# A decoder trunk in two layers on one core: 64 bytes of padding behind the constants, and with it every later tile in SBUF at another address

## The chip, the core and the metric

The kernel runs on one core of a Trainium2 chip. The metric is the device time of one execution in microseconds (us). The kernel before takes 2515.21 us, the median of three runs (2514.62 to 2516.56).

## What is computed

Two layers (DEPTH = 2) of a post-norm decoder over 256 tokens of width 2048, in float32:

```
h = x @ w_in                                  # 2048 -> 6704 columns
y = concat(hgrn2(h), nsa(h)) @ w_out          # two parallel head groups
x = LayerNorm(alpha * x + y)
f = (silu(gate) * up) @ w_down                # gate, up: causal depthwise conv of x @ w_up
x = LayerNorm(alpha * x + f)                  # w_up: 2048 -> 2*5632, w_down: 5632 -> 2048
```

Nearly all of the work is in the four products with weights. The two mixers (a gated linear recurrence and a sparse attention) run between the matmuls of `w_in`.

## The kernel before

Every weight is read from HBM once, in units of 128x1024 float32 (eight blocks of 128x128). SyncE loads a unit into `raw` (five buffers). ScalarE, or GpSimd for some units of `w_in`, rounds it to float32r as `whi` (`split`, L235 and L237), and VectorE writes the rest, `wlo` = `raw` - `whi` (L238); both have four buffers. Activations are held in the same two parts: `x` (16 blocks of 128x2x256), `o` (the mixers' outputs, in eight tiles of two blocks) and `f` (44 blocks). A block's first 256 columns are the high part and its next 256 the low part, so that they are 512 columns in a row.

`units` (from L300 on) makes the matmuls of one unit. For each of its eight blocks there is a matmul named **high** here (L325: 128x128 of `whi` as weights, all 512 columns of the activation's block moving) and one named **low** (L328: 128x128 of `wlo` as weights, the 256 columns of the high part moving):

```
mm(out, hi[:, o], x, start=k == 0, stop=False, ...)                        # L325, high
mm(st[c][:, 0], lo[:, 128 * i:128 * i + 128], act(k)[:, 0], ...)           # L328, low
```

Their order in a unit depends on `group`. In `w_up` and `w_down` it is 8: eight highs, then eight lows. In `w_in` and `w_out` it is 1: high, low, high, low. The first 12 units of `w_up` in each layer (6 column blocks, run side by side) have 2. The last column block of `w_out` and `w_down` takes two 256-column matmuls (L322) in place of a high. `w_in` has 80 such units a layer, `w_out` 32, `w_up` 176, `w_down` 88.

`tok_units` makes the value columns of `w_in` with the roles the other way round: 128x128 of `x` are the weights, and 512 columns (`w_v`) or 280 (`w_vg`) of `whi` or `wlo` move. It has three matmuls for each block and half of the tokens (L363, L364, L365), 12 a unit, and 16 units a layer of either width.

The order of the work on each engine, the buffers and the waits are settled when the program is built. Tiles come from pools that lie one behind the other in SBUF. The pool of constants holds `x`, `par`, `lbl`, `cf32`, `cb`, `lm`, `ones`, `eps`, `warm`, `half`, `lbt` and `lb`, in this order; a tile takes a multiple of 32 bytes of each partition. Behind it lies the pool of weights (`raw`, `whi`, `wlo`), and behind that the tiles of the stage: `o` and the mixers' work (`kh`, `q`, `hz` and others), or `f` and what the convolution and the norm need.

`lbt` is a small scratch tile in `load_consts`, used in a dozen short instructions at the start. Its rows 0 to 5 are used.

Of the kernel before, what the change touches and what calls it, by code (L numbers as in the profile page):

```python
# [29 lines left out]
F32 = mybir.dt.float32  # L30
# [73 lines left out]
class Trunk:  # L104
# [75 lines left out]
    def load_consts(self):  # L180
        nc, cp, a = self.nc, self.cp, self.a

        def ld(name, shape, dt):
            t = self.t(cp, shape, dt, name)
            self.after(nc.sync.dma_start(t, a[name]), self.load)
            return t

        self.after(self.load_par(0), self.load)
        self.lbl = ld("lbl", [128, L, 8], F32)
        self.cf = ld("cf32", [128, 673], F32)  # L190
        self.ident32 = self.cf[:, 641:673]
        self.cb = self.t(cp, [128, 416], BF16, "cb")
        self.lm = self.t(cp, [128, 80], U8, "lm")
        raw = self.t(self.wp, [128, 1024], F32, "raw", bufs=RAW_BUFS)
        self.after(nc.sync.dma_start(raw[:, :496], a["masks"]), self.load)
        nc.vector.tensor_copy(self.cb, raw[:, :416])
        nc.vector.tensor_copy(self.lm, raw[:, 416:496])
        self.ident = self.cf[:, 0:128]
        self.rc = self.cf[:, 128:384]
        self.rs = self.cf[:, 384:640]  # L200
        self.any = self.cf[:, 640:641]
        self.identb = self.cb[:, 0:128]
        self.caus = self.cb[:, 144:400]
        self.mask0 = self.cb[:, 128:416]
        self.ones = self.t(cp, [128, 128], F32, "ones")
        nc.gpsimd.memset(self.ones, 1.0 / D)
        self.eps = self.t(cp, [128, 3], F32, "eps")
        self.zero = self.eps[:, 2:3]
        nc.gpsimd.memset(self.zero, 0.0)
        self.warm = self.t(cp, [128, 1], F32, "warm")  # L210
        nc.gpsimd.memset(self.eps[:, 0:1], LN_EPS)
        nc.gpsimd.memset(self.eps[:, 1:2], RMS_EPS)
        self.half = self.t(cp, [128, 4], F32, "half")
        nc.gpsimd.memset(self.half, -0.5)

        v = nc.vector
        t = self.t(cp, [128, 6, 8], F32, "lbt")
        lb = self.lb = self.t(cp, [128, L, 2, 8], F32, "lb")
        v.tensor_max(t[:, 0], self.lbl[:, 0], self.lbl[:, 1])
        v.tensor_sub(t[:, 1], self.lbl[:, 0], t[:, 0])  # L220
        v.tensor_sub(t[:, 2], self.lbl[:, 1], t[:, 0])
        nc.scalar.activation(t[:, 1:3], t[:, 1:3], AF.Exp)
        v.tensor_add(t[:, 3], t[:, 1], t[:, 2])
        v.reciprocal(t[:, 3], t[:, 3])
        v.tensor_mul(t[:, 4], t[:, 1], t[:, 3])
        v.tensor_mul(t[:, 5], t[:, 2], t[:, 3])
        v.tensor_sub(lb[:, 0, 0], t[:, 4], t[:, 4])
        v.tensor_add(lb[:, 1, 0], t[:, 4], t[:, 5])
        v.tensor_sub(lb[:, 1, 0], lb[:, 1, 0], t[:, 4])
        for l in range(L):  # L230
            v.tensor_scalar(lb[:, l, 1], lb[:, l, 0], -1.0, 1.0, op0=ALU.mult, op1=ALU.add)
# [1109 lines left out]
```

## Time and profile before

| what | value |
|---|---|
| median of three runs | 2515.21 us (2514.62 to 2516.56) |
| the profiled execution's own time | 2517.57 us |
| its span, first to last instruction | 2515.8 us |
| mean granted TensorE clock | 0.993 of 2.4 GHz |
| TensorE matmuls (PE) busy | 2458.4 us, 98% of the span |
| weight loads (PEld) busy | 2121.2 us, 84% |
| VectorE (DVE) busy | 1781.0 us, 71% |
| ScalarE (ACT) busy | 1195.6 us, 48% |
| GpSimd (POOL) busy | 427.9 us, 17% |
| read from HBM | 432.20 MB, 173 GB/s over the span |

The profiled execution is 2.4 us above the median. PE's busy time joins matmuls that overlap in the pipeline, so a duration of one matmul says less than the distance from its start to the next one's start, which is what the timeline gives. In the timeline equal instructions that follow each other are one row with their count.

The stages of layer 0 lie at about 0 to 406 us (`w_in` with the mixers), 407 to 507 (`w_out` and the first norm), 513 to 998 (`w_up`) and 999 to 1247 (`w_down`); layer 1 repeats them about 1250 us later.

### The profile page before, as it was taken

To read this page: it belongs to the slowest core of one execution; us is meant where nothing else is said; L and a number is where in the kernel's file an instruction comes from. 1 tells how busy PE (TensorE), PEld (TensorE's weight loads), DVE (VectorE), ACT (ScalarE), POOL (GpSimd) and SP (SyncE) were. 2 spreads that over 40 slices of the span, in tenths; PEclk is the share of its full clock that TensorE was granted. 3 is DMA by queue.
4 is the path that set the end of the run, shared out by engine and by line. 5 is a ranking of instruction groups with operands and counts; after the bars stand their busy time and mean duration, and the time that the engine had idled before them with its cause. 6 is when DMAs were issued, how large, how long until landed. Compare 5 with 4: busy or idle time off the path is not lost.

```text
span 2515.8 us, 41290 instructions
## 1 busy us (share of the span) xinstructions
PE 2458.4 (98%) x15993; PEld 2121.2 (84%) x15993; DVE 1781.0 (71%) x2705; ACT 1195.6 (48%) x2189; POOL 427.9 (17%) x403
## 2 busy tenths in 40 slices
PE   8999999999999999999989999999999999999997
PEld 7788877888888888888878888788888888888887
DVE  7767876787777777555597678767977777775654
ACT  4144425465555555334331444354655555553343
POOL 0444551300000000001014445413000000000111
PEclk9999999999999999999999999999999999999999
DMA  6644343656666666665546443435565665655562
GB/s 234 212 156 142 119 147 122 184 168 193 192 190 190 192 192 192 186 191 185 159 156 206 154 135 126 142 127 176 176 193 190 190 191 192 193 188 190 178 199 101
DMA packets 122884, 436.99 MB, mean 174 GB/s; under 512 B 13760, under 2 KB 14528, under 8 KB 122688
## 3 DMA queue, kind: packets, MB, share of 16 engines
q1 hardware_dynamic: 122688, 434.35, 54.3%
q8 instruction: 126, 2.06, 0.3%
q14 instruction: 70, 0.57, 0.1%
HBM read 432.20 MB, written 2.10 MB: 173 GB/s over the span
## 4 chain that ended last, share of the span: by engine, by line
PE 87%; DVE 8%; issue 2%; ACT 1%; POOL 1%; DMA 1%; SPq 0%; ACTq 0%; POOLq 0%; DVEq 0%
PE pj L325 49%; PE pj L328 26%; DVE wlo L238 2%; PE pj L322 1%; PE pj L365 1%; PE pj L364 1%; PE t L325 1%; PE pj L363 1%; DVE rope L400 1%; PE h L657 1%; DMA raw<-w_in 1%; PE s L592 1%; PE s L513 1%; PE t L328 1%; DVE sg L447 1%
## 5 line engine op out<-in xcount | busy, mean ns | idle before, releaser
L238 DVE TENSOR_TENSOR wlo<-raw,whi 128x1024 fp32r<-128x1024 f32 (+2 forms) x819 | 1018.7, 1245 | 539.8 <-ACT whi L237 451.7
L325 PE MATMUL pj<-x,whi 128*128 128x512 f32 x3904 | 1117.7, 395 | 9.0 <-ACT whi L237 5.1
L237 ACT ACTIVATE whi<-raw 128x1024 fp32r<-128x1024 f32 (+2 forms) x631 | 661.7, 1049 | 796.1 <-PE pj L325 602.1
L325 PEld LDWEIGHTS pj<-x,whi 128*128 128x128 f32 x3904 | 709.0, 188 | 140.4 <-ACT whi L237 5.1
L328 PE MATMUL pj<-x,wlo 128*128 128x256 f32 x3904 | 715.6, 281 | 3.1 <-DVE wlo L238 3.1
L328 PEld LDWEIGHTS pj<-x,wlo 128*128 128x128 f32 x3904 | 592.1, 188 | 38.5 <-DVE wlo L238 4.4
L325 PE MATMUL pj<-f,whi 128*128 128x512 f32 x1320 | 331.2, 392 | 0.0
L235 POOL TENSOR_SCALAR whi<-raw 128x1024 fp32r<-128x1024 f32 (+1 forms) x188 | 217.7, 1160 | 330.9 <-PE pj L325 124.3
L325 PEld LDWEIGHTS pj<-f,whi 128*128 128x128 f32 x1320 | 237.3, 189 | 42.2
L828 POOL TENSOR_TENSOR s<-z 128x512 f32<-128x512 f32 x4 | 6.8, 1707 | 1182.2 <-DVE z L825 1182.2
L328 PEld LDWEIGHTS pj<-f,wlo 128*128 128x128 f32 x1408 | 191.7, 190 | 12.9
L328 PE MATMUL pj<-f,wlo 128*128 128x256 f32 x1408 | 197.6, 283 | 0.0
L1000 DVE SCALAR_TENSOR_TENSOR ct<-ch,par,ct 128x255 f32<-128x255 f32 (+1 forms) x352 | 167.8, 480 | 5.6
L325 PE MATMUL pj<-o,whi 128*128 128x512 f32 x480 | 168.5, 396 | 2.0 <-DVE o L600 1.9
L328 PE MATMUL pj<-o,wlo 128*128 128x256 f32 x512 | 143.5, 282 | 0.0
L325 PEld LDWEIGHTS pj<-o,whi 128*128 128x128 f32 x480 | 89.9, 188 | 23.8 <-DVE o L600 2.5
L998 ACT ACTIVATE ct<-ch,par 128x256 f32<-128x256 f32 x176 | 103.0, 587 | 0.0
L328 PEld LDWEIGHTS pj<-o,wlo 128*128 128x128 f32 x512 | 96.8, 189 | 0.4
L364 PE MATMUL pj<-wlo,x 128*128 128x280 f32 (+1 forms) x256 | 90.5, 355 | 5.6 <-DVE wlo L238 5.5
L363 PE MATMUL pj<-whi,x 128*128 128x280 f32 (+1 forms) x256 | 89.2, 355 | 2.3 <-POOL whi L235 2.3
L365 PE MATMUL pj<-whi,x 128*128 128x280 f32 (+1 forms) x256 | 90.7, 357 | 0.0
L375 DVE TENSOR_TENSOR ch<-pj,ch 128x256 f32<-128x256 f32 x170 | 70.9, 418 | 3.0 <-ACT ch L374 3.0
(248 smaller groups left out, 2249.2 us busy)
## 6 DMA issues: line engine op xcount, KB each, us to landing
raw<-w_up SPq DMA_DIRECT2D x352, 512.0 KB, 3.5
raw<-w_down SPq DMA_DIRECT2D x176, 512.0 KB, 3.6
raw<-w_in SPq DMA_DIRECT2D x158, 512.0 KB, 3.8
raw<-w_out SPq DMA_DIRECT2D x64, 512.0 KB, 3.6
raw<-w_v SPq DMA_DIRECT2D x32, 512.0 KB, 3.8
raw<-w_vg SPq DMA_DIRECT2D x32, 280.0 KB, 3.1
raw<-w_c SPq DMA_DIRECT2D x16, 512.0 KB, 3.6
out<-z SPq DMA_DIRECT2D x3, 512.0 KB, 2.6
```

Source lines behind the costliest of these rows:

```text
L235: self.nc.gpsimd.tensor_scalar(hi, raw, 1.0, 0.0, op0=ALU.mult, op1=ALU.add)
L237: self.nc.scalar.activation(hi, raw, AF.Copy)
L238: return self.nc.vector.tensor_sub(lo, raw, hi.bitcast(F32))
L322: mm(out[:, 0], hi[:, o], x[:, p], start=k == 0 and p == 0, stop=False, skip_group_check=True)
L325: mm(out, hi[:, o], x, start=k == 0, stop=False, skip_group_check=True)
L328: mm(st[c][:, 0], lo[:, 128 * i:128 * i + 128], act(k)[:, 0], start=False, stop=k == nk - 1, skip_group_check=True)
L363: mm(st[tt], xh, wh, start=first, stop=False, skip_group_check=True)
L364: mm(st[tt], xh, wl, start=False, stop=False, skip_group_check=True)
L365: mm(st[tt], xl, wh, start=False, stop=kt == KT - 1, skip_group_check=True)
L375: self.nc.vector.tensor_add(out, ps[:, 0], out)
L998: act(t[:, c], h[:, c], AF.Identity, scale=w[2], bias=w[3])
L1000: v.scalar_tensor_tensor(t[:, c, s:], h[:, c, :S - s], w[n], t[:, c, s:], op0=ALU.mult, op1=ALU.add)
```

## The change

The tile `lbt` gets two more rows that nothing reads or writes:

```
-        t = self.t(cp, [128, 6, 8], F32, "lbt")
+        t = self.t(cp, [128, 8, 8], F32, "lbt")
```

It grows from 192 to 256 bytes of each partition, so that every tile that is allocated behind it begins 64 bytes later. On each engine the instructions, their order and their waits are the same as before. Where the tiles begin, by the built program, in bytes of a partition:

| tile | before | behind a multiple of 128 by | after | behind a multiple of 128 by |
|---|---|---|---|---|
| `x` | 16512 | 0 | 16512 | 0 |
| `cf32` (with the identity) | 52832 | 96 | 52832 | 96 |
| `ones` | 56480 | 32 | 56480 | 32 |
| `raw`, first of five | 57408 | 64 | 57472 | 0 |
| `whi`, first of four | 77888 | 64 | 77952 | 0 |
| `wlo`, first of four | 94272 | 64 | 94336 | 0 |
| `o`, first tile, and `f` | 110656 | 64 | 110720 | 0 |
| `q`, first buffer | 198080 | 64 | 198144 | 0 |

The buffers of `raw`, `whi`, `wlo` and `o` are 4096 bytes each. A block of weights takes 512 bytes and a block of an activation 2048, so every block of a tile lies as its tile does against a multiple of 128. The distance from the weights to the moving columns, taken modulo 512 bytes, is 64 for `x` before and 0 after; for `o` and `f` it is 0 before and after.

## Rows read from the trace of the kernel before

**Rows 1.** The page: span, and each engine's busy us, share and instructions.
```profile
span 2515.8 us, 41290 instructions
PE 2458.4 (98%) x15993; PEld 2121.2 (84%) x15993; DVE 1781.0 (71%) x2705; ACT 1195.6 (48%) x2189; POOL 427.9 (17%) x403
```
**Rows 2.** The page: the chain that ended last, by engine, then by line.
```profile
PE 87%; DVE 8%; issue 2%; ACT 1%; POOL 1%; DMA 1%; SPq 0%; ACTq 0%; POOLq 0%; DVEq 0%
PE pj L325 49%; PE pj L328 26%; DVE wlo L238 2%; PE pj L322 1%; PE pj L365 1%; PE pj L364 1%; PE t L325 1%; PE pj L363 1%; DVE rope L400 1%; PE h L657 1%; DMA raw<-w_in 1%; PE s L592 1%; PE s L513 1%; PE t L328 1%; DVE sg L447 1%
```
**Rows 3.** Windows, layer 0: `w_out`, grouped part of `w_up`, `w_down`; columns in the first line.
```profile
core 0: us, PE busy (x) PEld busy (x) DVE busy (x) ACT busy (x) POOL busy (x), PEclk, DMA share, GB/s
...
407.00:507.00 100.00, 97.47 (x586) 85.01 (x585) 69.68 (x95) 46.11 (x59) 25.29 (x16) 1.00 0.54 168
...
546.00:998.00 452.00, 452.00 (x2623) 397.90 (x2622) 337.81 (x510) 267.18 (x424) 0.00 (x0) 1.00 0.61 192
1000.00:1247.00 247.00, 247.00 (x1461) 219.40 (x1460) 134.54 (x144) 98.65 (x99) 22.55 (x14) 1.00 0.60 187
```
**Rows 4.** Timeline, PE in `w_up`: start us, us to the last end, tiles, form, count.
```profile
701.14 1.99 PE L325 MATMUL pj<-x,whi 128*128 128x512 f32 x8
702.97 1.11 PE L328 MATMUL pj<-x,wlo 128*128 128x256 f32 x8
703.91 2.00 PE L325 MATMUL pj<-x,whi 128*128 128x512 f32 x8
705.75 1.07 PE L328 MATMUL pj<-x,wlo 128*128 128x256 f32 x8
706.65 1.99 PE L325 MATMUL pj<-x,whi 128*128 128x512 f32 x8
...
717.68 1.99 PE L325 MATMUL pj<-x,whi 128*128 128x512 f32 x8
```
**Rows 5.** Timeline, PE in `w_down`.
```profile
1102.21 2.00 PE L325 MATMUL pj<-f,whi 128*128 128x512 f32 x8
1104.05 1.12 PE L328 MATMUL pj<-f,wlo 128*128 128x256 f32 x8
1105.01 2.00 PE L325 MATMUL pj<-f,whi 128*128 128x512 f32 x8
...
1118.97 2.00 PE L325 MATMUL pj<-f,whi 128*128 128x512 f32 x8
```
**Rows 6.** Groups of weight loads: line, tiles, form, count, busy us, mean ns, idle.
```profile
L328 PEld LDWEIGHTS pj<-x,wlo 128*128 128x128 f32 x3904 | 592.1, 188 | 38.5 <-DVE wlo L238 4.4
...
L328 PEld LDWEIGHTS pj<-f,wlo 128*128 128x128 f32 x1408 | 191.7, 190 | 12.9
```
**Rows 7.** Timeline, PE in `w_out`: two highs, three pairs apart.
```profile
450.15 0.40 PE L325 MATMUL pj<-o,whi 128*128 128x512 f32 x1
...
451.21 0.40 PE L325 MATMUL pj<-o,whi 128*128 128x512 f32 x1
```
**Rows 8.** Timeline, PE in `w_in`: two highs, three pairs apart.
```profile
250.22 0.40 PE L325 MATMUL pj<-x,whi 128*128 128x512 f32 x1
...
251.28 0.40 PE L325 MATMUL pj<-x,whi 128*128 128x512 f32 x1
```
**Rows 9.** Timeline, PE in `w_v`: two matmuls, ten starts apart.
```profile
140.06 0.39 PE L365 MATMUL pj<-whi,x 128*128 128x512 f32 x1
...
142.40 0.39 PE L363 MATMUL pj<-whi,x 128*128 128x512 f32 x1
```
**Rows 10.** Groups by form: the first of three matmul lines of `tok_units`, both widths.
```profile
L363 PE MATMUL pj<-whi,x 128*128 128x512 f32 x128 | 52.3, 409 | 0.0
...
L363 PE MATMUL pj<-whi,x 128*128 128x280 f32 x128 | 36.9, 302 | 2.3 <-POOL whi L235 2.3
```
**Rows 11.** Groups of VectorE in `w_down`: an addition that reads `x`, one that does not.
```profile
L825 DVE SCALAR_TENSOR_TENSOR z<-x,z 128x256 f32<-128x256 f32 x8 | 3.4, 423 | 0.1
...
L824 DVE TENSOR_TENSOR z<-pj,z 128x256 f32<-128x256 f32 x8 | 3.4, 421 | 0.1
```

## The prediction

> **What bounds the kernel now.** I read the page first. The span is 2515.8 us and PE is busy for 98% of it [rows 1]. The chain that ended last says the same: 87% of it is PE, 49% the highs on `pj` (L325) and 26% the lows (L328), and only 8% is VectorE [rows 2]. So what counts is how closely matmuls follow each other. The windows show where nothing but that counts: in the grouped part of `w_up` and in `w_down` PE is busy for the whole stretch at a granted clock of 1.00, while VectorE is busy for 338 of 452 and 135 of 247 us, and the DMA engines for 0.61 and 0.60 of the time [rows 3]. Nothing else is late there, so a nanosecond more in the distance of two matmuls is a nanosecond more in the kernel.
>
> Then the timeline, for the distances. In `w_up` six groups of eight highs and eight lows take 717.68 - 701.14 = 16.54 us, 2.757 each [rows 4]. In `w_down` six groups take 1118.97 - 1102.21 = 16.76 us, 2.793 each [rows 5]. The instructions are of the same form in both, the weights come from the same buffers, the order in a group is the same, and PE waits for nothing in either. Yet a group costs 0.037 us more with `f` than with `x`. The lows differ most. With `x`, eight lows take 703.91 - 702.97 = 0.94 us in one group and 706.65 - 705.75 = 0.90 in the next [rows 4]; with `f` they take 0.96 [rows 5]. Their weight loads take 188 ns on average with `x`, and 190 with `f` [rows 6].
>
> Both the moving columns and the next weights are read from SBUF at the same time, and between the two stages only where the moving columns lie has changed: `x` lies 64 bytes from the weights (modulo 512), `f` 0 bytes. I take from this that the two reads get in each other's way, by an amount that hangs on their distance. That is a reading of two stages, not yet a proof.
>
> **The change part by part.** It adds no instruction, moves none and changes no wait. What it changes is addresses, and I go through who reads them.
>
> *w_up.* `x` stays and the weights move by 64 bytes, so that `x` comes to lie against its weights as `f` lies against them now, at distance 0. I price a group of `w_up` at a group of `w_down`: + 0.22 / 6 = 0.0367 us. There are 176 - 12 = 164 units in groups of eight a layer, 328 in all: 328 x 0.0367 = **+ 12.0 us**. All of it is on the path, as PE never idles there. The 24 units in groups of two have no counterpart with `f` or `o`; at the same 0.037 either way they are worth 0.9 us at most, and I take 0.
>
> *w_down.* `f` and the weights move together and their distance stays 0: **0 us**. If it is the place of `f` itself that costs, up to 0.037 a group comes back; that is a rival below.
>
> *w_out and w_in.* In `w_out` (distance 0) three pairs of high and low take 451.21 - 450.15 = 1.06 us [rows 7]; in `w_in` (distance 64) three pairs take 251.28 - 250.22 = 1.06 us [rows 8]. With highs and lows in turn the distance makes no difference that the rows show: **0 us**, with 0.01 us on three pairs either way, which over the 1280 pairs of `w_in` in both layers is 4.3 us.
>
> *The value columns.* Here `x` gives the weights and `whi` or `wlo` moves; the distance is 64 before, 0 after. Ten matmuls of 512 columns take 142.40 - 140.06 = 2.34 us, 0.234 each [rows 9]. At distance 0 the nearest row is the highs of `w_down`: 1104.05 - 1102.21 = 1.84 us for eight, 0.230 each [rows 5]. 3 x 128 matmuls of that width [rows 10] by 0.004 us are 1.5 us less; the 384 of 280 columns, priced by their width, 0.8 less. I take **- 2 us**. The bounds are 0 and - 3, the latter with the highs of `w_up`, 0.229 each [rows 4].
>
> *Everything else.* In the scores, the sums with `v` and the recurrence, both operands move together. The transposes and the sums with `ones` read one operand that stays, but they are few hundreds of short matmuls; I take 0, give or take 1 us. VectorE and ScalarE show no such effect: an addition that reads `x`, at a multiple of 128, takes 423 ns, and one of the same size that does not read it 421 [rows 11]. The loads into `raw` lie elsewhere too. No row shows one at a multiple of 128, but their queue has 0.39 of its time free in `w_up` [rows 3] and they run ahead of the work: 0 us, and the cover would have to go entirely before they cost anything.
>
> The sum is + 12 - 2 = **+ 10 us**. On the profiled execution that is 2517.57 + 10 = 2527.6; the median of the runs is 2.4 lower, so I forecast **2525 us**, with a range of its own of 2519 to 2531 (4.3 us for `w_in`, 0.9 and 1 for the small terms, and 1 for the value columns, of which I expect some to cancel).
>
> **Where the Trainium skill speaks against it.** The rows show matmuls of one form at distances that differ by stage, and weight loads that differ by 2 ns with them [rows 4 to 6]. The Trainium skill, in "SBUF — State Buffer", section "Who interferes with whom", says that TensorE has two read ports, one for the moving operand and one for weight loads, independent of each other, and that PE never waits on anyone. By that rule the sum is 0 and the time stays. The trace of before does not agree with it, as far as the difference of 0.037 us a group is one of addresses; no run so far moves an address alone.
>
> **The rivals.**
>
> *No change* (15%): the difference between `w_up` and `w_down` is not one of addresses, but of something else in which the stages differ, such as the place in the pattern at which a column block ends (16 blocks against 44) or VectorE's load, 75% against 54% [rows 3]. For it speaks that `w_in` and `w_out` cost the same [rows 7, 8] although their distances differ; against it, that the busier stage is the faster one. It gives 2515 us. The rule of the skill above gives the same.
>
> *The moving columns' own place counts* (18%): they are better read from a multiple of 128, as `x` is now, and the weights' place does not matter. Then `w_up` stays, and `w_down` gets its distance: 165 units (the last column block of 5.5 units a layer left out) x 0.0367 = 6.1 us less. The value columns come to 0.229 instead of 0.234: 384 x 0.005 = 1.9 less, and 1.0 for the narrower. That is - 9, 2506 us. For it: the value columns are at 64 behind a multiple of 128 and slow [rows 9], as `f` is. Against it: `o` is no slower than `x`.
>
> *Both aligned, hardly any conflict* (12%): no stage has both operands at a multiple of 128 now, so a state that no row shows is possible. Its best is bounded by the best of each kind: eight highs in 1.83 and eight lows in 0.90 [rows 4], a group at 2.73. `w_up` then gains 328 x 0.027 = 8.9 us, `w_down` 165 x 0.063 = 10.4, and the some 1790 pairs of `w_in` and `w_out`, from 0.353 to 0.342 (2.73 / 8), 20; the value columns 3. That is - 42, 2473 us.
>
> *A worse state* (12%): the same, on the other side. Highs as in the value columns, whose weights lie at a multiple of 128, 0.234 [rows 9], and lows as with `f`, 0.120 [rows 5], make a group of 2.83. `w_up` loses 328 x 0.073 = 24 us and `w_down` 165 x 0.037 = 6; a pair of `w_in` would be 0.354 and stay. That is + 30, 2545 us.
>
> **How the numbers follow.** The forecast has 43%. Its sign is decided in `w_up`: a group has to come out over 2.757 us by more than 0.015 for the kernel to be slower by 5 us, which is 0.2% and about what a measurement of this kernel can tell from no change. The range of 2502 to 2545 us takes in the forecast, no change, the moving columns' place and the worse state, and leaves out the 12% of a state without conflicts and some of the edges. Faster by over 0.2%: the 12% and most of the 18%, 0.28. Within 0.2%: the 15% and the edges of two others, 0.20. Slower: the forecast's rest and the worse state, 0.52.
>
> **What would show it.** If I am right, the timeline of `w_up` shows groups of 2.79 us with lows of 0.96, as `w_down` does before and after, and the weight loads of L328 with `x` rise from 188 to 190 ns; `w_in` and `w_out` keep 1.06 us for three pairs. If `w_down` falls to 2.757 and `w_up` stays, it was the moving columns' place. If a group of either stage lies below 2.74, distance is the wrong quantity altogether, and the place of the weights counts. If any difference shows on VectorE or in the loads rather than in PE's distances, the whole argument is beside the point.

## The result and the profile after

The changed kernel takes 2530.67 us, the median of four runs (2530.42 to 2533.06); the kernel before took 2515.23 beside it, also in four runs (2514.62 to 2516.56). The ratio is 1.0059, with a 95% interval of 1.0046 to 1.0071: slower by 0.59%, or 15.4 us (11.6 to 17.9 by the interval). The profiled execution took 2533.06 us, 2.4 above the median, as the profiled one of before did; it is the slowest of the four, with a granted clock of 0.990 where the other three have 0.992. Profile to profile the difference is 2531.3 - 2515.8 = 15.5 us, and it can be divided by stage. From the first matmul of a stage to the first of the next, and for `w_down` to the start of its own last matmul (us):

| stage | before, layer 0 | after | before, layer 1 | after | both layers |
|---|---|---|---|---|---|
| `w_in` | 401.54 | 404.84 | 400.98 | 402.71 | + 5.0 |
| `w_out` and first norm | 106.76 | 106.52 | 108.29 | 106.52 | - 2.0 |
| `w_up` | 485.43 | 491.64 | 485.43 | 491.64 | + 12.4 |
| `w_down` | 249.20 | 249.19 | 249.20 | 249.19 | 0.0 |

The page gives the same picture as [rows 1, 2]: the same instructions, the share of each engine the same to within 1%, and PE busier by 11 us.

```profile
span 2531.3 us, 41290 instructions
...
PE 2469.8 (98%) x15993; PEld 2135.7 (84%) x15993; DVE 1780.1 (70%) x2705; ACT 1196.4 (47%) x2189; POOL 428.1 (17%) x403
...
PE 87%; DVE 8%; issue 2%; DMA 1%; POOL 1%; ACT 1%; SPq 0%; ACTq 0%; POOLq 0%; DVEq 0%
```

VectorE, ScalarE and GpSimd are busy for the same time as before to within 1 us, so the addresses do nothing to them that the profile shows. The windows of `w_out`, of the grouped part of `w_up` and of `w_down` in layer 0 (columns as in [rows 3]) show the full clock, and in the last two a PE that never idles:

```profile
411.00:511.00 100.00, 97.15 (x585) 84.78 (x583) 70.00 (x96) 45.86 (x58) 25.23 (x16) 1.00 0.52 165
552.00:1002.00 450.00, 450.00 (x2580) 396.03 (x2579) 330.88 (x499) 261.87 (x415) 0.00 (x0) 1.00 0.60 190
1005.00:1252.00 247.00, 247.00 (x1450) 218.88 (x1449) 134.89 (x145) 100.39 (x103) 22.54 (x14) 1.00 0.58 186
```

The number of matmuls is the one to read: before, 452 us of `w_up` held 2623 of them, 5.80 a microsecond [rows 3]; now 450 us hold 2580, 5.73.

The timeline of PE in `w_up`, then in `w_down`:

```profile
700.93 2.00 PE L325 MATMUL pj<-x,whi 128*128 128x512 f32 x8
702.77 1.12 PE L328 MATMUL pj<-x,wlo 128*128 128x256 f32 x8
703.72 2.00 PE L325 MATMUL pj<-x,whi 128*128 128x512 f32 x8
705.56 1.12 PE L328 MATMUL pj<-x,wlo 128*128 128x256 f32 x8
706.52 2.00 PE L325 MATMUL pj<-x,whi 128*128 128x512 f32 x8
...
717.69 0.63 PE L325 MATMUL pj<-x,whi 128*128 128x512 f32 x2
...
1117.14 2.00 PE L325 MATMUL pj<-f,whi 128*128 128x512 f32 x8
1118.98 1.12 PE L328 MATMUL pj<-f,wlo 128*128 128x256 f32 x8
1119.93 2.00 PE L325 MATMUL pj<-f,whi 128*128 128x512 f32 x8
...
1133.90 1.32 PE L325 MATMUL pj<-f,whi 128*128 128x512 f32 x5
```

Six groups of `w_up` take 717.69 - 700.93 = 16.76 us, where they took 16.54 [rows 4]; six of `w_down` take 1133.90 - 1117.14 = 16.76, as before [rows 5]. `w_up` has become what `w_down` was: highs in 1.84 us, lows in 0.95. Over all 328 such groups the mean went from 2756.7 to 2793.2 ns, and the 158 of `w_down` stay at 2793.1. 328 x 0.0365 = 12.0 us of the 12.4; the other 0.4 are the units in groups of two. The weight loads of the lows with `x` went from 188 [rows 6] to 191 ns:

```profile
L328 PEld LDWEIGHTS pj<-x,wlo 128*128 128x128 f32 x3904 | 602.7, 191 | 35.9 <-DVE wlo L238 3.2
...
L328 PEld LDWEIGHTS pj<-f,wlo 128*128 128x128 f32 x1408 | 191.7, 190 | 12.9
```

In the three following pairs of timeline rows, three pairs of high and low in `w_out`, three in `w_in`, and ten value columns:

```profile
449.67 0.39 PE L325 MATMUL pj<-o,whi 128*128 128x512 f32 x1
...
450.71 0.39 PE L325 MATMUL pj<-o,whi 128*128 128x512 f32 x1
...
249.22 0.39 PE L325 MATMUL pj<-x,whi 128*128 128x512 f32 x1
...
250.26 0.39 PE L325 MATMUL pj<-x,whi 128*128 128x512 f32 x1
...
142.82 0.40 PE L363 MATMUL pj<-whi,x 128*128 128x512 f32 x1
...
145.11 0.39 PE L364 MATMUL pj<-wlo,x 128*128 128x512 f32 x1
```

1.04 us in both for three pairs, against 1.06 [rows 7, 8], and 2.29 us for ten value columns, against 2.34 [rows 9]. The matmuls of `w_in` follow each other a little more closely, and yet `w_in` is 5 us longer in this pair of executions. The windows show where the time lies: first the kernel after, then the kernel before.

```profile
60.00:80.00 20.00, 17.11 (x95) 14.43 (x94) 19.22 (x23) 6.58 (x14) 8.46 (x7) 0.90 0.69 222
100.00:120.00 20.00, 18.20 (x108) 15.38 (x107) 14.04 (x16) 2.52 (x8) 9.50 (x7) 0.91 0.71 231
140.00:160.00 20.00, 20.00 (x128) 16.41 (x128) 15.74 (x40) 14.29 (x45) 9.03 (x11) 0.93 0.44 139
360.00:380.00 20.00, 16.07 (x148) 11.93 (x151) 14.83 (x26) 6.82 (x22) 6.19 (x6) 0.83 0.34 108
```
```profile
60.00:80.00 20.00, 17.70 (x114) 14.88 (x111) 19.21 (x22) 6.28 (x14) 9.87 (x8) 1.00 0.69 225
100.00:120.00 20.00, 18.29 (x115) 15.29 (x114) 16.13 (x17) 2.90 (x9) 10.08 (x9) 1.00 0.70 238
140.00:160.00 20.00, 20.00 (x128) 15.91 (x128) 15.28 (x40) 15.01 (x49) 10.09 (x12) 1.00 0.48 155
360.00:380.00 20.00, 16.26 (x139) 12.07 (x140) 15.30 (x32) 7.00 (x23) 6.73 (x7) 0.91 0.38 123
```

A granted clock of 0.90 over 20 us is a stretch at 1.2 instead of 2.4 GHz, and (1 - 0.90) x 20 = 2.0 us is the most that it can cost. Together with the windows from 40 to 60 us (0.93 after, 0.91 before) and from 120 to 140 (0.98 and 1.00) that is at most 10.4 us after and 3.6 before, 6.8 more in layer 0. The lower clock stands behind places where PE had waited for its operands. The first place in the timeline at which the two kernels differ in this, after and before:

```profile
67.83 0.58 PE L328 MATMUL pj<-x,wlo 128*128 128x256 f32 x1 [2.90 <-DVE wlo L238]
```
```profile
67.48 0.39 PE L328 MATMUL pj<-x,wlo 128*128 128x256 f32 x1 [2.30 <-DVE wlo L238]
```

After a wait of 2.90 us the matmul takes 0.58 us, at half clock; after one of 2.30 it takes 0.39, at the full clock. The length of a wait does not decide it alone: early in `w_out` the kernel before has the same four waits in both layers, the longest 0.9 us, and a stretch at half clock among them in layer 1 only. In `w_in` of layer 1 both add to the time, the clock and the waits: at most 1.7 us more at the half clock, and 18.0 us without a matmul in `w_in`, where there were 14.1. Waits of PE between 1255 and 1660 us after, then between 1248 and 1654 before:

```profile
PE pj L325 <- POOL whi L235: 5.7, 2, 5.0
...
PE s L513 <- ACT o L517: 2.5, 2, 1.9
```
```profile
PE pj L325 <- POOL whi L235: 2.9, 2, 2.5
...
PE s L513 <- ACT o L517: 0.9, 2, 0.6
```

### The profile page after: what moved, and what is told of

Read it like the earlier page. It is cut to its first block, busy times and chain, and to the rows that moved or that the text cites. A ratio compares the mean times of both kernels' runs of the same rounds, so it can differ in the third digit from the quotient of the medians.

```text
span 2531.3 us, 41290 instructions
## 1 busy us (share of the span) xinstructions
PE 2469.8 (98%) x15993; PEld 2135.7 (84%) x15993; DVE 1780.1 (70%) x2705; ACT 1196.4 (47%) x2189; POOL 428.1 (17%) x403
## 4 chain that ended last, share of the span: by engine, by line
PE 87%; DVE 8%; issue 2%; DMA 1%; POOL 1%; ACT 1%; SPq 0%; ACTq 0%; POOLq 0%; DVEq 0%
PE pj L325 49%; PE pj L328 26%; DVE wlo L238 2%; PE pj L322 1%; PE t L325 1%; PE pj L364 1%; PE pj L365 1%; PE pj L363 1%; DVE rope L400 1%; PE h L657 1%; DMA raw<-w_in 1%; POOL whi L235 1%; PE s L592 1%; PE s L513 1%; DMA raw<-w_vg 1%
## 5 line engine op out<-in xcount | busy, mean ns | idle before, releaser
L328 PE MATMUL pj<-x,wlo 128*128 128x256 f32 x3904 | 725.0, 284 | 2.9 <-DVE wlo L238 2.9
L328 PEld LDWEIGHTS pj<-x,wlo 128*128 128x128 f32 x3904 | 602.7, 191 | 35.9 <-DVE wlo L238 3.2
```

## The experiments

Distance means the start of the activation's block minus the start of the weights, modulo 512 bytes. Each kernel has the same 41290 instructions; only tiles move. Each was timed beside the kernel before on the same chip (2517.82, 2516.84, 2518.2 and 2518.11 us in the four sessions: medians of 9 runs in the first and 13 in the last, one run in the other two). A time without a number of runs is that of one run. Times of stages and groups come from one profiled execution of each kernel. "Group" is the mean, in ns, over all 328 groups of eight highs and eight lows in `w_up`, or 158 in `w_down`.

**1. Both operands, or the distance between them?** The change moved the weights *and* set the distance of `x` to 0. `x` gets 64 unused bytes ahead of it, which moves it and all that lies behind; the second kernel adds the change itself.

```
-  self.x = self.t(self.cp, [128, KT, 2, S], F32R, "x")
+  self.x = self.t(self.cp, [128, 16 + KT * 2 * S], F32R, "x")[:, 16:].rearrange("p (k h t) -> p k h t", h=2, t=S)
```

Weights at a multiple of 128 as after, `x` 64 behind, distance 64 (`x` only moved):

> Everything behind and including x lies 64 bytes later than in the kernel before: the weights lie at a multiple of 128 as in the changed kernel, x at 64 behind one, and the distance from weights to x is 64 again. Theory of the distance: w_up goes back to 2.757 us a group with lows of 0.94 and 0.90, w_down stays at 2.793, about 2515 us. Theory of the weights' place: w_up stays at 2.793 as in the changed kernel, about 2530 us. Theory of x's place (a multiple of 128 is better for what moves): w_up at 2.79 or above, 2530 us or more.

Measured: 2515.84 us, `w_up` 485.43 and 485.47 us, group 2756.7; `w_in` 401.35 and 401.25 us, as before the change.

`x` and weights both 64 behind a multiple of 128, distance 0 (`x` moved, `lbt` with 8 rows):

> x lies 64 bytes later than in the kernel before and the weights 128 later, so that both are at 64 behind a multiple of 128 and the distance is 0. Theory of the distance: w_up at 2.793 us a group, as in the changed kernel, about 2530 us. Theory of the weights' place: w_up at 2.757, about 2515 us. With the run before it, all four pairs of places have then been seen.

Measured: 2531.99 us, `w_up` 491.67 us in both layers, group 2793.2; `w_in` 403.57 and 401.82 us. A group of each in the timeline, `x` only moved first:

```profile
700.20 1.99 PE L325 MATMUL pj<-x,whi 128*128 128x512 f32 x8
702.02 1.11 PE L328 MATMUL pj<-x,wlo 128*128 128x256 f32 x8
702.97 1.31 PE L325 MATMUL pj<-x,whi 128*128 128x512 f32 x5
```
```profile
700.01 2.00 PE L325 MATMUL pj<-x,whi 128*128 128x512 f32 x8
701.85 1.11 PE L328 MATMUL pj<-x,wlo 128*128 128x256 f32 x8
702.80 1.55 PE L325 MATMUL pj<-x,whi 128*128 128x512 f32 x6
```

2.77 us and 2.79; one group alone shows it badly, as its cost at distance 64 alternates, and the mean over 328 shows it well. With the two kernels of the case this makes four corners: weights at 64 or 0, `x` at 64 or 0. The cost goes with the distance in all four, and with neither place. The weights' place and the activation's place both fall as causes.

**2. The same in `w_down`.** `f` gets 64 bytes ahead of it (the same edit as for `x`, at the line that makes `f`); with it moves only what its stage allocates behind it.

> The kernel before with f alone moved by 64 bytes (and what its stage allocates behind it). Theory of the distance: w_down falls from 2.793 to 2.757 us a group, 165 groups x 0.0367 = 6 us less, 2509 us, faster than both kernels; w_up stays. If it were the stage that makes w_down slower (where column blocks end, VectorE's load), it stays at 2.793 and the time at 2515 us.

Measured: 2510.32 us, median of six (2508.53 to 2511.95), 0.9967 of the kernel before (0.9955 to 0.9980). `w_down` takes 246.00 us a layer, 3.2 less, and its group 2757.0; `w_up` stays at 485.43. This kernel is faster than both. A group of `w_down`:

```profile
1104.02 1.99 PE L325 MATMUL pj<-f,whi 128*128 128x512 f32 x8
1105.85 1.11 PE L328 MATMUL pj<-f,wlo 128*128 128x256 f32 x8
1106.79 0.39 PE L325 MATMUL pj<-f,whi 128*128 128x512 f32 x1
```

The tile that moves is now the activation, and the price of 64 bytes is the same, 0.036 us a group. The rival by which the stages differ in something else than addresses has fallen with this.

**3. Which distances are cheap?** `x` 32 and `f` 96 (`lbt` with 7 rows, 96 bytes ahead of `f`):

> Weights 32 bytes later than in the kernel before, f 96 behind its place against them: distance 32 for x, 96 for f, 0 for o. No theory has a number for these. If only 64 bytes matter, w_up and w_down each show either 2.757 or 2.793 us a group; if the effect is finer, other sums of lows and highs show up, between 2.72 (no conflict) and 2.84. Together with no change of w_out, 2495 to 2545 us.

Measured: 2540.00 us; `w_up` 492.68 us with a group of 2800.0, `w_down` 251.96 with 2826.5. `x` -64 and `f` 128 (`lbt` with 10 rows, 128 bytes ahead of `f`):

> Weights 128 bytes later than in the kernel before, f a further 128: the distance is -64 for x and 128 for f. If only the distance modulo 128 counts, every group is as before: w_up 2.757 us (highs 227.5, 230.4, 228.8 ns in turn), w_down 2.793, about 2516 us. If it counts modulo 256 or more, both stages show sums not seen yet.

Measured: 2524.49 us; group 2773.3 with `x`, 2810.1 with `f`. -64 and 64 differ by 128 bytes and by 17 ns, 0 and 128 by 17 ns as well: the pattern does not repeat after 128 bytes. `x` 48 and `f` 16 (16 bytes ahead of each):

> Distance 48 for x and 16 for f, 0 for o: x begins 16 bytes later in its tile, the weights 32 later, f 16 later in its tile. So far a group costs 2.793 us at 0, 2.800 at 32, 2.757 at 64 and 2.837 at 96. If the cost runs smoothly with the distance, 48 gives about 2.78 and 16 about 2.80. If 16 bytes decide, values outside of 2.75 to 2.84 turn up, perhaps under 2.757, which would be a better place than any seen.

Measured: 2536.95 us; group 2806.7 with `x`, 2786.2 with `f`. `x` -16 and `f` 80 (16 bytes ahead of `x`, `lbt` with 8 rows, 80 ahead of `f`):

> Distance -16 (112) for x and 80 for f, 0 for o: x begins 16 bytes later in its tile, the weights 96 later, f 80 later in its tile. If the cost runs smoothly with the distance, 112 gives about 2.815 us a group and 80 about 2.80, some 2535 to 2545 us in all. If 16 bytes decide, other values, perhaps under 2.757.

Measured: 2531.35 us; group 2806.7 with `x`, 2799.8 with `f`. In order of distance, eight highs and eight lows apart (ns):

| distance | -64 | -16 | 0 | 16 | 32 | 48 | 64 | 80 | 96 | 128 |
|---|---|---|---|---|---|---|---|---|---|---|
| highs | 1861.7 | 1865.8 | 1840.7 | 1853.1 | 1866.8 | 1863.3 | 1831.3 | 1849.1 | 1867.4 | 1861.2 |
| lows | 911.7 | 940.8 | 952.5 | 933.1 | 933.2 | 943.3 | 925.4 | 950.7 | 959.1 | 948.8 |
| group | 2773.3 | 2806.7 | 2793.2 | 2786.2 | 2800.0 | 2806.7 | 2756.7 | 2799.8 | 2826.5 | 2810.1 |

There is no smooth course. Distance 64, where `x` lay before, is the cheapest of the ten; each shift tried here that took `x` away from it made `w_up` longer. Where an expectation has another price for one of these distances (2.837 us a group at 96, lows of 0.907 at -64, highs of 1.845 at 0), the table is the mean over all groups and the better number.

**4. A distance of its own for highs and lows.** Highs are cheapest at 64, lows at -64. A gap of 64 bytes between the buffers of `whi` and of `wlo` (and `lbt` with 8 rows) gives `x` 0 to `whi` and -64 to `wlo`, and `f` and `o` 64 to `whi` and 0 to `wlo`. For the lows of `x` the expectation has the sign wrong: against the kernel before, `wlo` moves by 128 bytes and `x` stays, and 64 - 128 = -64.

> 64 bytes more ahead of whi, and 64 more between whi and wlo: for x the distance is 0 to whi and 64 to wlo, for f and o 64 to whi and 0 to wlo. If each kind of matmul pays by the distance to its own weights: w_up 1.841 for the highs as at distance 0 and 0.925 for the lows as at 64, a group at 2.765; w_down 1.831 and 0.953, at 2.784; about 2517 us. If the highs leave a state to the lows, the sums differ from these by 0.01 us or more.

Measured: 2527.06 us; group 2780.1 with `x` (lows 942.5) and 2790.4 with `f` (lows 951.1). The lows of `x`, at -64, did not get the 912 ns that they take where the highs are at -64 too: after highs at distance 0 they are dearer. What pays is `w_out`, with 104.65 us in place of 106.76: most pairs take 340 ns (340.7 on average), where the average before was 350. `w_in` was slow, 407.43 us in layer 0, with more of the half clock than in any other kernel.

Next, each stage its own place inside buffers that are 512 bytes longer. Room for them came from a smaller scratch of the DMA queues, so that `x` and all behind it lie 8192 bytes lower and the weights' buffers 4608 apart, both multiples of 512. 64 unused bytes ahead of `o` and ahead of `f` bring these to distance 64 as well. `AT` has the places of `whi` and `wlo` in their buffers, in elements of 4 bytes: 0 leaves the distance at 64, 16 makes it 0, and 32 makes it -64.

```
+AT = dict(w_in=(0, 16), tok=(16, 16), w_out=(0, 16), w_up=(0, 32), w_down=(16, 32))
...
-                    hi = self.t(self.wp, [128, 1024], F32R, "whi", bufs=PART_BUFS)
-                    lo = self.t(self.wp, [128, 1024], F32R, "wlo", bufs=PART_BUFS)
+                    hi, lo = (self.t(self.wp, [128, ROOM], F32R, tag, bufs=PART_BUFS)[:, a:a + 1024]
+                              for tag, a in zip(("whi", "wlo"), units[ns][3].__defaults__[-1]))
```

> Each stage gets its own two distances (moving operand minus weights, for whi and for wlo): w_in 64 and 0, value columns 0, w_out 64 and 0, w_up 64 and -64, w_down 0 and -64. If highs and lows each keep the cost seen at their own distance, a group of 16 of w_up costs 1.831 + 0.907 = 2.738 us (before 2.757), one of w_down 1.845 + 0.907 = 2.752 (before 2.793), the pairs of w_out 340 ns (w_out 104.6 us a layer): -6 -7 -6 against the kernel before, and -2 from the value columns, 2496 us, between 2490 and 2505 with the half-clock stretches of w_in. If what the highs leave to the lows matters as much as in the kernel with 0 and 64, each group is 15 to 20 ns dearer and the kernel comes to 2500 to 2510. If the distance of each kind has no cost of its own, w_up stays at 2.757 or above.

Measured: 2502.36 us, beside 2518.2 before. `w_up` 484.1 us, group 2747.0 (highs 1835.2, lows 911.8); `w_down` 248.00, group 2780.0 (highs 1838.0, lows 942.0); `w_in` 398.78 and 398.48; `w_out` 104.79 and 105.39. The expectation of 2496 counted on lows of 907 in `w_down`, and missed; its second case, 2500 to 2510, came in. With the sign right the kernel before this one had shown it: `x` in that one and `f` in this one both lie at 0 and -64, and a group takes 2780.1 and 2780.0. The second kernel has other numbers in `AT`: `w_in` and the value columns (0, 0), `w_out` (0, 32), `w_up` (32, 0), `w_down` (0, 32).

> Distances for whi and wlo: w_in 64 and 64 as before, w_out 64 and -64, w_up -64 and 64, w_down 64 and -64. If highs and lows each keep the cost seen at their own distance, w_up costs 1.867 + 0.925 = 2.792 us a group (+11 us over the two layers against before), w_down 2.738 (-10 us), and w_out is unlike 350 ns a pair by what 64 and -64 bring: 2510 to 2520 in all. If the lows take over what the highs leave, w_up lies nearer 2.773 (both at -64), and w_down above 2.757. w_down of this kernel against w_up of the other (64 and -64 in both) tells whether the stage itself matters: it should not.

Measured: 2525.17 us; `w_up` at -64 and 64 has a group of 2803.3 (highs 1860.8, lows 942.5), `w_down` at 64 and -64 one of 2749.1 (highs 1836.1, lows 913.0) and 244.92 us a layer. These results and the table read together: lows at -64 take 912 to 913 ns behind highs at 64 or at -64, and 942 to 943 behind highs at 0; lows at 64 take 925 behind highs at 64, and 942.5 behind highs at -64. Lows at 0 take 951 to 953 behind highs at 64 or 0. Highs keep their cost to within 8 ns whatever the lows have, which is less than the 30 ns of the lows but not much less than the 9.4 ns between highs at 0 and at 64. So a high's cost follows mostly its own distance, while a low's also depends on what the highs before it had. And the stage does not matter: `w_up` and `w_down` with the same two distances cost the same to 2 ns (2747.0 and 2749.1 at 64 and -64; at 0 and -64 to 0.1 ns).

**5. Is the extra time of `w_in` that of its distance?** Only the weights of `w_in` and of the value columns move, to distance 0: `AT` has (16, 16) for these two and (0, 0) for the rest, and there are no unused bytes ahead of `o` and `f`.

> Only the weights of w_in and of the value columns move, so that x lies at distance 0 from them as in the changed kernel; w_out, w_up and w_down keep their distances of before. If the extra time of w_in in the changed kernel (404.84 and 402.71 us against 401.54 and 400.98) belongs to the distance in w_in itself, this kernel shows about 404 and 402.5 us there, several half-clock stretches more than before, w_up at 485.43 and w_down at 249.20, and comes out 3 to 6 us above before. If it belongs to the places of the other tiles (what VectorE and ScalarE read and write), w_in comes out at 399 to 401 us, because its value columns are faster, and the kernel 1 to 4 us below before.

Measured: 2518.10 us, median of ten (2514.47 to 2520.22), 1.0001 of the kernel before (0.9992 to 1.0011). In the profiled execution, the fastest of the ten, `w_in` takes 400.82 and 400.06 us, 0.7 and 0.9 less than before, and two windows of before and after read:

```profile
60.00:80.00 20.00, 17.74 (x111) 14.87 (x107) 19.21 (x23) 6.69 (x15) 10.19 (x8) 1.00 0.72 225
100.00:120.00 20.00, 18.16 (x115) 15.12 (x114) 16.44 (x17) 2.91 (x9) 9.82 (x8) 1.00 0.72 236
```

Clock 1.00, as before the change and unlike after it. Group 2756.7 in `w_up` and 2793.1 in `w_down`, as before, so the new room in the buffers and the smaller scratch do nothing there. The distance in `w_in` makes the whole kernel neither slower nor, by the median, faster; the interval leaves 2.0 us less to 2.8 more. By the expectation this leaves the places of the other tiles, but experiment 1 speaks against these: in its first kernel all tiles from `raw` on lie where they lie in the changed one, and `w_in` takes 401.35 and 401.25 us. In its second, with `x` at distance 0 as after the change and everything 64 bytes further on, it takes 403.57 and 401.82, in layer 0 again with more of the half clock than before. So in these executions neither the distance in `w_in` nor those places made it longer alone. Why `w_in` takes 5 us more in the changed kernel stays open; the course of the waits, which begins differently when the matmuls before are faster, was not tried alone.

**6. The cheapest distance everywhere.** `AT` as in the first kernel of part 4, but `w_down` with (0, 32).

> For every stage the distances that were cheapest so far: w_in 64 to whi and 0 to wlo, value columns 0, w_out 64 and 0, w_up 64 and -64, w_down 64 and -64. It is the kernel with w_down at 0 and -64 (2502.36 us), with w_down at 244.92 us in place of 248.00 a layer, as the kernel with w_down at 64 and -64 showed: 2502.4 - 6.2 = 2496 us, between 2493 and 2500 with the half-clock stretches of w_in, 0.8% below before. If the order of the places in one stage shifted the next stage's cost, w_up would leave 2746.7 ns a group or w_in 398.8 us.

Measured: 2497.67 us, median of four (2496.03 to 2499.21), 0.9920 of the kernel before (0.9905 to 0.9935). `w_in` 399.42 and 398.35 us, `w_out` 105.4, `w_up` 484.1, `w_down` 244.80. A group of `w_up`, and three pairs in `w_out`:

```profile
700.14 2.00 PE L325 MATMUL pj<-x,whi 128*128 128x512 f32 x8
701.98 1.07 PE L328 MATMUL pj<-x,wlo 128*128 128x256 f32 x8
702.89 1.30 PE L325 MATMUL pj<-x,whi 128*128 128x512 f32 x5
...
448.13 0.39 PE L325 MATMUL pj<-o,whi 128*128 128x512 f32 x1
...
449.15 0.39 PE L325 MATMUL pj<-o,whi 128*128 128x512 f32 x1
```

2.75 us a group and 1.02 us for three pairs, as short as any seen. It lies 20 us below the kernel before, and the changed one lies 15 above it, with the same instructions.

## Why the prediction was right, and where it was not

*What bounds it: right.* In `w_up` and `w_down` nothing but the spacing of PE's starts set the time, so that 36.5 ns a group came through in full.

*w_up, + 12.0 us: right.* + 12.4 measured, of which 12.0 are the 328 groups. Pricing a group at distance 0 by the stage that had it already worked to a nanosecond, because what repeats is a fixed pattern: `x` at distance 0 takes the very distances of starts that `f` took. The quantity named, the distance of the two operands and not the place of either, holds in the four corners of experiment 1 and, with the activation moved, in experiment 2. The prediction called it a reading of two stages; it is shown now. That the two reads get in each other's way is not shown: the runs show the spacing by distance, and not what in the hardware makes it.

*w_down, 0: right.* 249.19 us against 249.20.

*w_out, 0: right.* The three pairs shown went from 1.06 to 1.04 us, but over the whole of `w_out` in layer 0 a pair went only from 350.2 to 349.3 ns on average, some 0.2 us a layer. The other 1.5 of the 2.0 us lie in layer 1, where the trace before has a stretch at half clock (0.91 between 1660 and 1680 us, at most 1.8 us) and the trace after has none; no step of the prediction bears on it, and that it came off the time is luck.

*The value columns and w_in, - 2 us with 4.3 either way: wrong by 7 in this pair of executions.* The matmuls did what the step said and a little more: value columns of 512 went from 233.2 to 228.8 ns on average, pairs of high and low from 352 to 350. That is 192 x 4.4 ns = 0.8 us for the wide ones, 192 x 0.5 ns = 0.1 for the narrow ones (129.0 to 128.5 ns, far less than the share by width that the prediction gave them), and 640 x 2 ns = 1.3 us for the pairs: 2.2 us a layer, 4.4 in all. But `w_in` came out 5.0 us longer. The step that failed is the term of the value columns, "I take **- 2 us**": it let the saving through to the end, although in `w_in` PE idles and waits, unlike in `w_up`. There a faster matmul only reaches its next wait earlier. In layer 0 PE was without work for 16.9 us both times, and up to 6.8 us went to the half clock behind the waits; in layer 1 it was 3.9 us more of idle time and up to 1.7 of the half clock. As bounds these are 6.8 - 2.2 = 4.6 us and 3.9 + 1.7 - 2.2 = 3.4, and measured were 3.3 and 1.7. By the medians `w_up` has 12.4 of 15.4 us, so that `w_in` and `w_out` together have 3.0, with -0.8 to 5.5 by the interval: the saving of 2 us did not arrive, but how much `w_in` lost is known only roughly. Experiments 1 and 5 show neither the distance in `w_in` nor the places of the tiles to do it alone; what does remains open, and with it whether these 5 us would stay under another small change.

*The sum.* The parts forecast were 12.0 and -2, the parts measured 12.4 and 5.0, with -2.0 from `w_out` that had been put at 0; 2525 forecast, 2530.67 measured. It lies in the range that the forecast had for itself, 2519 to 2531, but at its edge, on account of `w_in`; that `w_out` gave back 2.0 of the 5.0 us in the pair of profiles is luck.

*The rivals.* "No change" is out by the result. By the Trainium skill, "SBUF — State Buffer", section "Who interferes with whom", the moving operand and the weight load have independent read ports and PE never waits on anyone; the traces here do not agree that the time stays, with 2756.7 against 2793.2 ns a group by an address alone. "The moving columns' own place" is out by experiment 1, "both aligned, hardly any conflict" by the groups of 2.79 us. "A worse state" did not come to be at distance 0, but is to be had: distances of 32, 48 and -16 bytes take groups of 2.80 to 2.81, and 96 takes 2.83, the price that the rival was given. (2.73 / 8 is 0.341, not 0.342; the rival without conflicts would have come out 1 to 2 us lower.)

## What to carry to other kernels

Where a profile shows PE busy throughout and two stages with the same instructions differ by a per cent or two, compare the addresses of what moves with those of the weights, before looking for a cause in the schedule; unused bytes ahead of one tile tell within one run, and here measuring a handful of distances did better than a multiple of 128 for everything, which is the changed kernel. A tile that is added in front shifts every later one; here 64 bytes that nobody reads cost 0.59%. Write the distance down with its sign and take it from the addresses of the built program: one wrong sign cost a forecast here. A saving came through at its full price only in the stages where PE never waits; in `w_in`, which has waits, faster matmuls came out as 5 us more in one kernel, and in another as no change of the whole time.

## What the runs showed of the hardware that was not expected

- How closely matmuls of one form are started varies by 2.9% with the distance of their two operands in SBUF: the same 16 matmuls took from 2746.7 ns (64 to `whi`, -64 to `wlo`) to 2826.5 (96 to both). Steps of 16 bytes matter, and 128 bytes are not a period.
- The cost is not of one matmul alone: eight lows at -64 took 912 ns behind highs at 64 or -64, and 942 behind highs at 0.
- In groups of eight the pattern belongs to the distance: in the changed kernel and in the one with `x` and the weights both moved, the 328 groups have the same mean, 2793.2 ns, at different addresses. With highs and lows in turn it does not: in the kernel with only `x` moved, a pair of `w_out` takes 347.0 ns on average in layer 0 and 352.3 in layer 1, at the same addresses.
- A wait of 2.90 us was followed by a stretch of PE at half clock, and one of 2.30 at the same place was not; the same short waits in `w_out` had one among them in one layer and none in the other. The ten runs of experiment 5 spread over 5.7 us, with mean granted clocks of 0.991 to 0.993, so a difference of a few microseconds between two single runs says little about a change.
